# The delta rule's gates raised in priority, head 0's work scheduled right behind them, and a longer delay before its inverse

## The chip, the cores and the metric

The kernel runs on one NeuronCore of a Trainium2 chip. The metric is device time in microseconds (us), the median over executions; lower is better. Engines are named as in the profile: PE is TensorE's matmul stream, PEld its weight loads, DVE is VectorE, ACT is ScalarE, POOL is GpSimd, SP is SyncE (here it only issues DMAs).

## What is computed

A differential-attention layer, then a feed-forward block, a token mixer and a second feed-forward block, on 512 tokens of 1024 features in float32. The change lies in the token mixer, in its gated delta rule of eight heads (head size 128). The part that matters, with the sizes of this case (T = 512, H = 8):

```
proj = h @ mix_w_in                     # xp, q, k, v, z, b_raw, a_raw, g_pool, g_dn
qkv  = silu(causal_depthwise_conv([q, k, v]))          # 4 taps
beta = sigmoid(b_raw)                                  # T x H
g    = -exp(a_log) * softplus(a_raw + dt_bias)         # T x H
gc   = cumsum(g)                                       # within a chunk
decay = exp(gc_i - gc_j), lower triangle
a_mat = strict lower part of beta_i * (k_i . k_j) * decay
sol   = inverse(a_mat + I) applied to [beta*v, beta*exp(gc)*k]
for each chunk:  v_new = u - w S;  o = q_dec S + qk v_new;  S = S exp(g_last) + k_dec^T v_new
```

So every head needs the gates `beta` and `gc` of all heads, then a triangular inverse, then a scan over four chunks of 128 tokens.

## The kernel before

Everything is laid out by hand on PE: each wide product is split in high and low parts (`whi`, `wlo`, made from a `raw` weight tile by `split`, line 105: ACT casts `whi`, DVE subtracts to get `wlo`), and `mm3` issues three matmuls per 128 rows. A column of a projection (`gemm_col`, line 187) is 24 matmuls of 128x512 that write one PSUM bank. In the mixer these columns are the filler: while PE streams them, the small steps of the delta rule are put in between.

What decides the order: the class has a planner's clock, `self.now`, in us. Each matmul adds its planned time; `later(delay, fn)` puts a step on a heap, due that long after the present; `spend` runs what is due after each group of three matmuls; `run_until(cond)` runs steps at once until a condition holds. The delays are the numbers in `DL` (line 34): `cs` from the first gate steps to the cumulative sum, `U` from the solved diagonal blocks to the inverse's first level, `pr` from the end of a head's columns to that head. PE runs its instructions exactly in the order in which they are written. DVE, ACT and POOL are arranged by the library's scheduler by priority when the program is built; what `high_priority(offset=PRIO)` encloses is moved ahead of it by 200. On the chip each engine runs its row of instructions in that fixed order.

The steps that the change touches, by line:

- `ev_ba` and `ba_trans` (lines 984 to 1036): the b and a columns are turned by four small matmuls (line 992, `sc<-ident,ba`); ACT takes an exponential (998); DVE adds, inverts and clips (999 to 1004); POOL takes a power of 32 numbers per partition (1006); then 21 DVE operations on 128x32 numbers build the logarithm's series and the gate `y` (1008 to 1019). The tile is `gwork`.
- `cumsum` (1021): one small product of `y` with a triangle on PE (`sc<-gwork,cst`), copied to `gc` by DVE (1024). `rows` (1028): `gc` is turned on PE (`sc<-ident,gc`), copied (1032) and written to DRAM by a DMA that POOL issues (1033).
- `delta(h)` (1062): `decays` reads a row of that back (`row`), and makes `E` and `ET` on DVE and POOL; `products` turns k and q on PE (`sc<-ident,cvy`); POOL works out the head's factors from `ssqk` (1103 to 1110, `b` among them); `products2` multiplies k by k (`sc<-cvy`) and scales it into `E` (DVE 1119); `substitution` solves the 16x16 diagonal blocks on DVE: 15 shuffles (1153), 15 steps of `pr` and `xs` (1161, 1163), then `U` (1169). `inverse` (1175) joins blocks in three levels, each with `sc<-U,E`, a DVE step to `Q` (1186), `sc<-Q,X`, and a DVE update of `U` (1195).
- The convolution of each head's q, k and v: three DVE operations per column (1048, `cvy<-cvr,cols,cvy`).
- The loop over heads at the end of `mixer` (1317 to 1331): head 0's columns come from `gemm_quad`; `zcol(0)` and four columns of another gate (`gcol`, the "extra products", `EXTRA[0] = 4`) follow; then, for head 0 only, `run_until(gates)`, and each head is put on the heap 18 us later.

Of the kernel before, what the change touches and what calls it, by code (L numbers as in the profile page):

```python
# [15 lines left out]
P = 128  # L16
# [17 lines left out]
DL = dict(ada=21.24, qk=11.18, p0=10.0, wt=6.0, o=14.0, U=10.0, hn=7.73, lev=3.5, ch=2.2, cs=25.33, po=13.74, pr=18.0, T=3.17, la=6, gs=4, gp=5, Ts=6.12, P2=150)  # L34
# [7 lines left out]
class Net:  # L42
# [912 lines left out]
    def mixer(self):  # L955
# [33 lines left out]
        def ba_trans(ba):  # L989
# [5 lines left out]
            work = self.tile("gwork")  # L995
            e, y, m, t1, t2, ser, eb = (work[:, 32 * i:32 * i + 32].rearrange("p (h t) -> p h t", t=NT) for i in range(7))
            ea = work[:, 224:232]
            nc.scalar.activation(e, v[:, 0:8, :], AF.Exp, scale=-1.0)
            nc.vector.tensor_scalar(e, e, 1.0, None, op0=ALU.add)
            nc.vector.reciprocal(beta, e)  # L1000
# [4 lines left out]
            nc.vector.memset(eb, math.e)  # L1005
            nc.gpsimd.tensor_tensor(e, eb, t1, op=ALU.pow)

            nc.vector.tensor_scalar(t1, e, 2.0, None, op0=ALU.add)
            nc.vector.reciprocal(t2, t1)
            nc.vector.tensor_tensor(t1, e, t2, op=ALU.mult)  # L1010
# [7 lines left out]
            nc.gpsimd.tensor_tensor(ea, work[:, 192:200], alog, op=ALU.pow)  # L1018
            nc.vector.scalar_tensor_tensor(y, y, -1.0, ea.unsqueeze(2).broadcast_to([P, H, NT]), op0=ALU.mult, op1=ALU.mult)

            def cumsum():
                cs = self.bank("sc")
                self.mm(cs[:, :32], tri, fl(y))
                nc.vector.tensor_copy(fl(gc), cs[:, :32])
                nc.scalar.activation(egc, gc, AF.Exp)
                self.later(1.0, rows)

            def rows():
                tr2 = self.bank("sc")
                nc.tensor.transpose(tr2[:32, :P], fl(gc), self.ident)  # L1030
                gt = self.tile("gt")
                nc.vector.tensor_copy(gt[:32, :P], tr2[:32, :P])
                nc.gpsimd.dma_start(gdram.rearrange("h (t n) -> (h t) n", n=P), gt[:32, :P])
                st["gates"] = True

            self.later(DL["cs"], cumsum)


# [23 lines left out]
        def delta(h):  # L1062
# [75 lines left out]
            def substitution():  # L1138
# [27 lines left out]
                def expand():  # L1166
# [5 lines left out]
                    self.later(DL["U"], lambda: inverse(0))  # L1172
# [148 lines left out]
        for h in range(H):  # L1321
# [6 lines left out]
            if h == 0:  # L1328
                self.run_until(lambda: st["gates"])
            self.later(DL["pr"], lambda h=h: delta(h))  # L1330
# [120 lines left out]
```

## Time and profile before

| | |
|---|---|
| median of 3 runs | 1855.97 us (1852.57 to 1855.99) |
| the profiled execution | 1854.37 us, of which 1852.6 us are its span |
| PE busy | 1811.6 us, 98% of the span |
| DVE / ACT / POOL busy | 76% / 50% / 22% |
| the mixer's delta rule | about 960 to 1360 us of the span |

A timeline row gives the start in us, the duration, the engine, the line, the operation, the tiles as out<-in, and, in brackets, how long the engine had been idle and what released it. Neighbouring instructions of one kind are merged in a row (x2 and so on); durations of matmuls overlap, so a merged row's length is not a sum. PEclk is the granted TensorE clock: 1.00 is 2.4 GHz, 0.50 is 1.2 GHz.

### The profile page before, as it was taken

What the parts mean: (1) busy time and instruction counts of PE and PEld (TensorE: products, weight loads), DVE (VectorE), ACT (ScalarE), POOL (GpSimd) and SP (SyncE); (2) the same over time, 40 slices, a digit from 0 to 9 for tenths busy, and PEclk for the clock granted to TensorE, in tenths of its full rate; (3) what the DMA queues carried; (4) which work ended last, traced back from release to release, by engine and by line L of the source; (5) the groups of instructions that cost most, each with busy time, mean ns of one, the idle gap of its engine ahead of it and who ended that gap; (6) DMA issues with size and microseconds to landing.
All of it is one profiled execution on the core that took longest, in us unless ns stands there. A gap on an engine that the chain in (4) does not pass through costs nothing. (4 is left out here: it accounts for less than half of the span.)

```text
span 1852.6 us, 29069 instructions
## 1 busy us (share of the span) xinstructions
PE 1811.6 (98%) x10799; PEld 1598.0 (86%) x10799; DVE 1405.9 (76%) x2904; ACT 934.2 (50%) x1696; POOL 409.2 (22%) x396
## 2 busy tenths in 40 slices
PE   8999999999999999999999999999999999999997
PEld 5888888888888999998898778888888899999886
DVE  5558777777856899998365798787868789999833
ACT  5576676475743544453245745654433254445421
POOL 3213124042102123232030212212110022322201
PEclk9999999999999999999999999999999999999999
DMA  4535544535422233357324321222357323333731
GB/s 171 136 107 144 161 120 126 188 92 154 133 86 73 69 115 95 112 187 234 114 62 121 88 65 52 63 63 77 100 170 231 117 69 114 94 113 103 228 103 57
DMA packets 186594, 217.93 MB, mean 118 GB/s; under 512 B 9619, under 2 KB 129827, under 8 KB 186453
## 3 DMA queue, kind: packets, MB, share of 16 engines
q1 hardware_dynamic: 178864, 192.68, 34.6%
q0 software_dynamic: 6864, 22.27, 3.9%
q8 instruction: 85, 1.39, 0.3%
q10 hardware_dynamic: 724, 1.12, 0.2%
q14 instruction: 57, 0.46, 0.1%
HBM read 201.34 MB, written 2.11 MB: 110 GB/s over the span
## 5 line engine op out<-in xcount | busy, mean ns | idle before, releaser
L84 PE MATMUL acc<-hT,whi 128*128 128x256 f32 (+1 forms) x2704 | 639.9, 330 | 0.6 <-DVE hT L107 0.5
L84 PEld LDWEIGHTS acc<-hT,whi 128*128 128x128 f32 x2704 | 445.5, 191 | 33.4 <-DVE hT L107 0.7
L84 PE MATMUL acc<-hT,wlo 128*128 128x256 f32 (+1 forms) x1352 | 440.3, 326 | 3.0 <-DVE wlo L107 2.9
L106 ACT CAST whi<-raw 128x1024 fp32r<-128x1024 f32 (+1 forms) x325 | 285.7, 880 | 296.3 <-PE acc L84 232.2
L107 DVE TENSOR_TENSOR wlo<-raw,whi 128x1024 fp32r<-128x1024 f32 (+1 forms) x325 | 330.5, 1027 | 132.1 <-ACT whi L106 130.6
L84 PEld LDWEIGHTS acc<-hT,wlo 128*128 128x128 f32 x1352 | 257.5, 190 | 26.1 <-DVE wlo L107 4.2
L84 PE MATMUL acc<-whi,hT 128*128 128x512 f32 x768 | 264.9, 403 | 1.9 <-ACT hT L106 1.9
L84 PE MATMUL acc<-whi,gs 128*128 128x512 f32 x704 | 219.6, 390 | 1.6 <-DVE gs L107 1.6
L305 POOL TENSOR_TENSOR rs<-ms,mhalf 128x8 f32<-128x8 f32 (+2 forms) x60 | 86.2, 1438 | 447.5 <-DVE ms L303 388.0
L84 PE MATMUL acc<-T,whi 128*128 128x256 f32 x960 | 174.5, 283 | 0.0
L84 PEld LDWEIGHTS acc<-whi,hT 128*128 128x128 f32 x768 | 144.1, 188 | 32.1 <-ACT hT L106 2.9
L84 PEld LDWEIGHTS acc<-whi,gs 128*128 128x128 f32 x704 | 132.0, 188 | 29.9 <-DVE gs L107 2.5
L106 ACT CAST whi<-S 128x512 fp32r<-128x512 f32 x160 | 99.4, 621 | 115.2 <-DVE S L232 87.7
L84 PE MATMUL acc<-wlo,hT 128*128 128x512 f32 x384 | 150.5, 392 | 2.8 <-DVE wlo L584 2.8
L84 PEld LDWEIGHTS acc<-T,whi 128*128 128x128 f32 x960 | 149.8, 192 | 0.0
L107 DVE TENSOR_TENSOR wlo<-S,whi 128x512 fp32r<-128x512 f32 x160 | 140.1, 895 | 0.2 <-ACT whi L106 0.2
L84 PE MATMUL acc<-wlo,gs 128*128 128x512 f32 x352 | 137.1, 389 | 0.0
L84 PE MATMUL acc<-T,wlo 128*128 128x256 f32 x480 | 135.8, 283 | 0.0
L232 POOL TENSOR_TENSOR S<-raw,S 128x512 f32<-128x512 f32 x40 | 65.7, 1643 | 200.7 <-DVE S L232 158.6
L780 ACT ACTIVATE p<-p,mn 128x128 f32<-128x128 f32 (+3 forms) x128 | 71.1, 557 | 48.8 <-DVE mn L776 48.2
L84 PEld LDWEIGHTS acc<-T,wlo 128*128 128x128 f32 x480 | 92.2, 192 | 0.0
L84 PEld LDWEIGHTS acc<-wlo,hT 128*128 128x128 f32 x384 | 72.5, 189 | 14.7 <-DVE wlo L584 3.7
(299 smaller groups left out, 3113.6 us busy)
## 6 DMA issues: line engine op xcount, KB each, us to landing
raw<-in_ffn_w_in_dram SPq DMA_DIRECT2D x88, 512.0 KB, 3.6
raw<-in_l_w_in_dram SPq DMA_DIRECT2D x60, 512.0 KB, 4.1
raw<-in_mix_w_in_dram SPq DMA_DIRECT2D x53, 512.0 KB, 3.9
araw<-in_ada_w_dram SPq DMA_DIRECT2D x96, 256.0 KB, 4.3
raw<-in_ffn_w_out_dram SPq DMA_DIRECT2D x44, 512.0 KB, 3.7
ada<-in_ada_w_dram POOLq DMA_DIRECT2D x48, 256.0 KB, 4.2
raw<-in_l_w_out_dram SPq DMA_DIRECT2D x16, 512.0 KB, 3.7
ab<-in_ada_b_dram POOLq DMA_DIRECT2D x18, 256.0 KB, 4.2
```

Of the source, the lines that this page charges most:

```text
L84: self.nc.tensor.matmul(out, a, b, start=start, stop=stop, skip_group_check=onto)
L106: return (self.nc.scalar.copy(hi, src), self.nc.vector.tensor_tensor(lo, src, hi.bitcast(F32), op=ALU.subtract))
L107: self.nc.vector.tensor_tensor(lo, src, hi.bitcast(F32), op=ALU.subtract))
L232: sub = lambda o, x, y, op=ALU.subtract, e=nc.vector: e.tensor_tensor(o, x, y, op=op)
L305: pin(nc.gpsimd.tensor_tensor(r[:, :n], ms[:, :n], self.mhalf[:, :n], op=ALU.pow))
L780: nc.scalar.activation(p_[m][:, :L], p_[m][:, :L], AF.Exp, bias=mn[:, m:m + 1], scale=-1.0, accum_out=st[:, m, b:b + 1])
```

## The change

The gate steps of `ba_trans` become a function `logs` whose body is run at high priority; the power's result goes to a tile part of its own (`x`), so that the DVE steps for `beta` move behind the power's issue; two preparations (a memset and another power) move ahead of the projection. `cumsum` and `rows` keep their PE steps at ordinary place and get high priority for the copies. `cs` falls from 25.33 to 14.0. Head 0 no longer waits for the end of the extra products: `rows` itself puts `delta(0)` on the heap 5 us later (`d0`). Head 0's delay from solved blocks to inverse is 18 (`U0`) in place of 10. Nothing is computed anew or left out. Each old line 999 to 1019 has its counterpart at 1009 to 1028; other lines in the mixer move down by 11.

```diff
@@ -31,7 +31,7 @@
 SLOTS = 61
 PRIO = 200
 
-DL = dict(ada=21.24, qk=11.18, p0=10.0, wt=6.0, o=14.0, U=10.0, hn=7.73, lev=3.5, ch=2.2, cs=25.33, po=13.74, pr=18.0, T=3.17, la=6, gs=4, gp=5, Ts=6.12, P2=150)
+DL = dict(ada=21.24, qk=11.18, p0=10.0, wt=6.0, o=14.0, U=10.0, hn=7.73, lev=3.5, ch=2.2, cs=14.0, d0=5.0, U0=18.0, po=13.74, pr=18.0, T=3.17, la=6, gs=4, gp=5, Ts=6.12, P2=150)
 
 
 ORDER = ["M1", "M4", "M7", "M6", "M5", "M2", "M3"]
@@ -992,22 +992,32 @@
                 nc.tensor.transpose(tr[:, t * 16:(t + 1) * 16], ba[:16, sl(t)], self.ident[:16, :16])
             self.now += 0.2
             v = tr[:, :64].rearrange("p (t c) -> p c t", c=16)
-            work = self.tile("gwork")
-            e, y, m, t1, t2, ser, eb = (work[:, 32 * i:32 * i + 32].rearrange("p (h t) -> p h t", t=NT) for i in range(7))
-            ea = work[:, 224:232]
+            with self.tc.high_priority(offset=PRIO):
+                y = logs(v)
+            self.later(DL["cs"], lambda: cumsum(y))
+
+        gwork = self.tile("gwork")
+        e, y_, m, t1, t2, ser, eb = (gwork[:, 32 * i:32 * i + 32].rearrange("p (h t) -> p h t", t=NT) for i in range(7))
+        ea = gwork[:, 224:232]
+        nc.vector.memset(eb, math.e)
+        nc.gpsimd.tensor_tensor(ea, gwork[:, 192:200], alog, op=ALU.pow)
+
+        def logs(v):
+
+            y = y_
             nc.scalar.activation(e, v[:, 0:8, :], AF.Exp, scale=-1.0)
-            nc.vector.tensor_scalar(e, e, 1.0, None, op0=ALU.add)
-            nc.vector.reciprocal(beta, e)
             nc.vector.tensor_tensor(y, v[:, 8:16, :], dtb.unsqueeze(2).broadcast_to([P, H, NT]), op=ALU.add)
             nc.vector.tensor_scalar(t1, y, 0.0, None, op0=ALU.min)
             nc.vector.tensor_scalar(m, y, 0.0, None, op0=ALU.max)
             nc.vector.tensor_tensor(t1, t1, m, op=ALU.subtract)
-            nc.vector.memset(eb, math.e)
-            nc.gpsimd.tensor_tensor(e, eb, t1, op=ALU.pow)
-
-            nc.vector.tensor_scalar(t1, e, 2.0, None, op0=ALU.add)
-            nc.vector.reciprocal(t2, t1)
-            nc.vector.tensor_tensor(t1, e, t2, op=ALU.mult)
+            x = t2
+            nc.gpsimd.tensor_tensor(x, eb, t1, op=ALU.pow)
+            nc.vector.tensor_scalar(e, e, 1.0, None, op0=ALU.add)
+            nc.vector.reciprocal(beta, e)
+
+            nc.vector.tensor_scalar(t1, x, 2.0, None, op0=ALU.add)
+            nc.vector.reciprocal(e, t1)
+            nc.vector.tensor_tensor(t1, x, e, op=ALU.mult)
             nc.vector.tensor_tensor(t2, t1, t1, op=ALU.mult)
             nc.vector.tensor_scalar(ser, t2, 2.0 / 17, 2.0 / 15, op0=ALU.mult, op1=ALU.add)
             for d in (13, 11, 9, 7, 5, 3, 1):
@@ -1015,25 +1025,26 @@
                 nc.vector.tensor_scalar(ser, ser, 2.0 / d, None, op0=ALU.add)
             nc.vector.tensor_tensor(ser, ser, t1, op=ALU.mult)
             nc.vector.tensor_tensor(y, ser, m, op=ALU.add)
-            nc.gpsimd.tensor_tensor(ea, work[:, 192:200], alog, op=ALU.pow)
             nc.vector.scalar_tensor_tensor(y, y, -1.0, ea.unsqueeze(2).broadcast_to([P, H, NT]), op0=ALU.mult, op1=ALU.mult)
-
-            def cumsum():
-                cs = self.bank("sc")
-                self.mm(cs[:, :32], tri, fl(y))
+            return y
+
+        def cumsum(y):
+            cs = self.bank("sc")
+            self.mm(cs[:, :32], tri, fl(y))
+            with self.tc.high_priority(offset=PRIO):
                 nc.vector.tensor_copy(fl(gc), cs[:, :32])
                 nc.scalar.activation(egc, gc, AF.Exp)
-                self.later(1.0, rows)
-
-            def rows():
-                tr2 = self.bank("sc")
-                nc.tensor.transpose(tr2[:32, :P], fl(gc), self.ident)
-                gt = self.tile("gt")
+            self.later(1.0, rows)
+
+        def rows():
+            tr2 = self.bank("sc")
+            nc.tensor.transpose(tr2[:32, :P], fl(gc), self.ident)
+            gt = self.tile("gt")
+            with self.tc.high_priority(offset=PRIO):
                 nc.vector.tensor_copy(gt[:32, :P], tr2[:32, :P])
-                nc.gpsimd.dma_start(gdram.rearrange("h (t n) -> (h t) n", n=P), gt[:32, :P])
-                st["gates"] = True
-
-            self.later(DL["cs"], cumsum)
+            nc.gpsimd.dma_start(gdram.rearrange("h (t n) -> (h t) n", n=P), gt[:32, :P])
+            st["gates"] = True
+            self.later(DL["d0"], lambda: delta(0))
 
 
         conv_out = {}
@@ -1169,7 +1180,7 @@
                     nc.vector.tensor_tensor(U.rearrange("p (t b i) -> p t b i", t=NT, b=8), b8(xs, 2),
                                             b8(bmask.rearrange("p (b i) -> p b i", b=8), 1), op=ALU.mult)
                     d["U"] = U
-                    self.later(DL["U"], lambda: inverse(0))
+                    self.later(DL["U"] if h else DL["U0"], lambda: inverse(0))
 
                 self.later(2.0, lambda: shuffles(0))
 
@@ -1325,9 +1336,8 @@
                 zcol(h)
             for _ in range(EXTRA[h]):
                 rest.pop(0)()
-            if h == 0:
-                self.run_until(lambda: st["gates"])
-            self.later(DL["pr"], lambda h=h: delta(h))
+            if h:
+                self.later(DL["pr"], lambda h=h: delta(h))
         for f in rest[:-KD]:
             f()
         self.ada(1, 2, 2.5)
```

In the built program the rows of PE, DVE, ACT and POOL differ only in the mixer. Three places are shown.

PE, the small steps of the gates and of head 0 (`sc_..<-gwork` is the cumulative sum, `sc_..<-ident,gc` the turn of `gc`, `cvy` are k and q of a head, `U` its blocks; the wide matmuls between them are left out). Before:

```order
L84 MATMUL sc_10457<-gwork_10218,cst_10008 128x32
...
L1030 MATMUL sc_10467<-ident_75,gc_10017 32x128
...
L95 MATMUL sc_10706<-ident_75,cvy_10294 128x128 x4
L95 MATMUL sc_10716<-ident_75,cvy_10262 128x128 x4
...
L84 MATMUL sc_10762<-cvy_10294 128x128 x4
L84 MATMUL sc_10780<-cvy_10262,cvy_10294 128x128 x4
...
L95 MATMUL sc_10986<-ident_75,cvy_10578 128x128 x4
...
L84 MATMUL sc_11081<-U_10954,E_10645 128x4x16 x4
```

After:

```order
L84 MATMUL sc_10388<-gwork_10020,cst_10008 128x32
...
L1041 MATMUL sc_10398<-ident_75,gc_10017 32x128
...
L95 MATMUL sc_10509<-ident_75,cvy_10294 128x128 x4
L95 MATMUL sc_10519<-ident_75,cvy_10262 128x128 x4
...
L84 MATMUL sc_10550<-cvy_10294 128x128 x4
L84 MATMUL sc_10568<-cvy_10262,cvy_10294 128x128 x4
...
L84 MATMUL sc_10859<-U_10734,E_10438 128x4x16 x4
...
L95 MATMUL sc_11027<-ident_75,cvy_10718 128x128 x4
```

The cumulative sum stands 51 wide matmuls earlier than before, inside the first extra column in place of the third. Head 0's turns stand 57 wide matmuls behind the turn of `gc` (141 before). Between them and the first use of `U` stand 153 wide matmuls (105 before), and head 1's turns (`cvy_10718`, before `cvy_10578`) now follow that use. From head 1's turns to the first use of its own `U` there are 87 wide matmuls (93 before).

DVE, the gate chain (`gwork`) from the power's result on, with convolution taps (`cvy`) and weight splits (`wlo`) of the columns between. Before:

```order
L1004 TENSOR_TENSOR gwork_10218<-gwork_10218 128x32
L1048 SCALAR_TENSOR_TENSOR cvy_10262<-cvr_10260,cols_87,cvy_10262 128x511
L1008 TENSOR_SCALAR gwork_10218<-gwork_10218 128x32
L1048 SCALAR_TENSOR_TENSOR cvy_10262<-cvr_10260,cols_87,cvy_10262 128x510
L1009 RECIPROCAL gwork_10218<-gwork_10218 128x32
L1048 SCALAR_TENSOR_TENSOR cvy_10262<-cvr_10260,cols_87,cvy_10262 128x509
L1010 TENSOR_TENSOR gwork_10218<-gwork_10218 128x32
L107 TENSOR_TENSOR wlo_10369<-raw_10366,whi_10368 128x1024
L1011 TENSOR_TENSOR gwork_10218<-gwork_10218 128x32
L107 TENSOR_TENSOR wlo_10402<-raw_10399,whi_10401 128x1024
```

After:

```order
L1012 TENSOR_TENSOR gwork_10020<-gwork_10020 128x32
L1018 TENSOR_SCALAR gwork_10020<-gwork_10020 128x32
L1059 SCALAR_TENSOR_TENSOR cvy_10262<-cvr_10260,cols_87,cvy_10262 128x511
L1019 RECIPROCAL gwork_10020<-gwork_10020 128x32
L1059 SCALAR_TENSOR_TENSOR cvy_10262<-cvr_10260,cols_87,cvy_10262 128x510
L1020 TENSOR_TENSOR gwork_10020<-gwork_10020 128x32
L107 TENSOR_TENSOR wlo_10369<-raw_10366,whi_10368 128x1024
L1021 TENSOR_TENSOR gwork_10020<-gwork_10020 128x32
L1059 SCALAR_TENSOR_TENSOR cvy_10262<-cvr_10260,cols_87,cvy_10262 128x509
L1022 TENSOR_SCALAR gwork_10020<-gwork_10020 128x32
```

The first tap (128x511) has moved behind the step that takes the power's result (1008, now 1018). From that step to the gate's last step (1019, now 1028) the row still holds other work between the chain's steps: nine taps and four splits, where it held eight taps and four splits.

DVE, head 1's first level and the head behind it (`Q0` and `U_11241`, after `U_11279`, are head 1's; `E_11222`, after `E_11249`, and what follows it are head 2's). Before:

```order
L1119 SCALAR_TENSOR_TENSOR E_11222<-sc_11355,b2_11321,E_11222 128x128 x4
L1123 TENSOR_TENSOR ET_11223<-sc_11373,ET_11223 128x512
L1142 TENSOR_TENSOR abd_11364<-E_11222,cst_10008 128x512
L1125 TENSOR_TENSOR kd_11379<-kt_11304,ekd_11226 128x512
L1144 TENSOR_REDUCE Ac_11366<-abd_11364 128x64
L1126 TENSOR_TENSOR kt_11304<-kt_11304,bB_11322 128x512
L1186 TENSOR_TENSOR Q0_10010<-sc_11382,cst_10008 128x16x16
L1195 TENSOR_TENSOR U_10954<-U_10954,sc_11395 128x4x64
L1153 STREAM_SHUFFLE La_11368<-Ac_11366 128x64 x7
L1153 STREAM_SHUFFLE La_11369<-Ac_11366 128x64 x4
L1195 TENSOR_TENSOR U_11241<-U_11241,sc_11437 128x16x16
```

After:

```order
L1197 TENSOR_TENSOR Q0_10010<-sc_11417,cst_10008 128x16x16
L1130 SCALAR_TENSOR_TENSOR E_11249<-sc_11390,b2_11361,E_11249 128x128 x4
L1239 SCALAR_TENSOR_TENSOR S_11434<-S_11336,egl_10450,av_11432 128x128
L1153 TENSOR_TENSOR abd_11399<-E_11249,cst_10008 128x512
L1136 TENSOR_TENSOR kd_11414<-kt_11344,ekd_11253 128x512
L1155 TENSOR_REDUCE Ac_11401<-abd_11399 128x64
L1137 TENSOR_TENSOR kt_11344<-kt_11344,bB_11362 128x512
L1164 STREAM_SHUFFLE La_11403<-Ac_11401 128x64 x7
L1164 STREAM_SHUFFLE La_11404<-Ac_11401 128x64 x4
L1206 TENSOR_TENSOR U_11279<-U_11279,sc_11474 128x16x16
```

Head 1's `Q0` now stands ahead of head 2's `E` rows, and its update of `U` still behind them.

## Rows read from the trace of the kernel before

**Rows 1.** The page: busy time of each engine.

```profile
PE 1811.6 (98%) x10799; PEld 1598.0 (86%) x10799; DVE 1405.9 (76%) x2904; ACT 934.2 (50%) x1696; POOL 409.2 (22%) x396
```

**Rows 2.** Stretches of 20 us: length, busy time by engine, granted clock, DMA.

```profile
core 0: us, PE busy (x) PEld busy (x) DVE busy (x) ACT busy (x) POOL busy (x), PEclk, DMA share, GB/s
980.00:1000.00 20.00, 20.00 (x91) 16.46 (x90) 7.52 (x15) 10.55 (x13) 1.13 (x2) 1.00 0.56 146
1000.00:1020.00 20.00, 20.00 (x90) 16.56 (x89) 10.66 (x14) 10.59 (x14) 1.28 (x2) 1.00 0.35 97
1040.00:1060.00 20.00, 17.25 (x93) 14.52 (x92) 19.30 (x54) 15.56 (x23) 3.56 (x2) 0.96 0.53 143
1060.00:1080.00 20.00, 17.86 (x82) 14.77 (x81) 17.16 (x78) 8.06 (x15) 3.68 (x7) 0.87 0.19 55
1080.00:1100.00 20.00, 18.09 (x118) 15.90 (x117) 17.27 (x68) 11.92 (x22) 4.91 (x8) 1.00 0.14 41
```

**Rows 3.** PE's timeline at the waits of heads 0 and 1.

```profile
1039.27 0.50 PE L84 MATMUL acc<-hT,wlo 128*128 128x512 f32 x1 [1.01 <-DVE wlo L107]
...
1056.74 1.08 PE L84 MATMUL sc<-U,E 128*128 128x64 f32 x8 [2.68 <-DVE U L1169]
...
1059.08 1.20 PE L84 MATMUL acc<-hT,whi 128*128 128x512 f32 x2
...
1061.79 0.64 PE L84 MATMUL acc<-hT,whi 128*128 128x512 f32 x2
...
1071.20 1.22 PE L84 MATMUL sc<-U,E 128*128 128x64 f32 x8 [2.14 <-DVE U L1195]
...
1072.93 1.20 PE L84 MATMUL acc<-hT,whi 128*128 128x512 f32 x2
...
1075.57 0.62 PE L84 MATMUL acc<-hT,whi 128*128 128x512 f32 x2
...
1096.14 1.08 PE L84 MATMUL sc<-Q,X 128*128 128x64 f32 x8 [1.91 <-DVE Q L1186]
```

**Rows 4.** Two stretches of 3.4 us behind these waits, as rows 2.

```profile
1058.40:1061.80 3.40, 3.40 (x11) 2.81 (x12) 1.84 (x4) 2.02 (x4) 1.44 (x1) 0.50 0.56 154
1072.05:1075.45 3.40, 3.40 (x13) 2.92 (x13) 3.40 (x12) 0.51 (x1) 0.00 (x0) 0.50 0.54 144
```

**Rows 5.** PE's timeline at the cumulative sum.

```profile
989.18 0.30 PE L84 MATMUL sc<-gwork,cst 128*128 128x32 f32 x2
```

**Rows 6.** POOL's timeline: the power in the gate chain.

```profile
963.75 5.43 POOL L1006 TENSOR_TENSOR gwork<-gwork 128x32 f32<-128x32 f32 x1 [6.56 <-DVE gwork L1004]
```

**Rows 7.** DVE's timeline: the gate chain.

```profile
962.98 0.35 DVE L1000 RECIPROCAL beta<-gwork 128x32 f32<-128x32 f32 x1
...
963.48 0.19 DVE L1004 TENSOR_TENSOR gwork<-gwork 128x32 f32<-128x32 f32 x1
964.40 0.75 DVE L1048 SCALAR_TENSOR_TENSOR cvy<-cvr,cols,cvy 128x511 f32<-128x511 f32 x1 [0.73 <-ACT cvy L1046]
969.22 0.18 DVE L1008 TENSOR_SCALAR gwork<-gwork 128x32 f32<-128x32 f32 x1 [4.07 <-POOL gwork L1006]
969.31 0.74 DVE L1048 SCALAR_TENSOR_TENSOR cvy<-cvr,cols,cvy 128x510 f32<-128x510 f32 x1
969.97 0.35 DVE L1009 RECIPROCAL gwork<-gwork 128x32 f32<-128x32 f32 x1
...
981.82 0.19 DVE L1016 TENSOR_TENSOR gwork<-gwork 128x32 f32<-128x32 f32 x1
982.05 0.19 DVE L1017 TENSOR_TENSOR gwork<-gwork 128x32 f32<-128x32 f32 x1
982.28 0.19 DVE L1019 SCALAR_TENSOR_TENSOR gwork<-gwork 128x32 f32<-128x32 f32 x1
```

**Rows 8.** DVE's timeline: head 1's shuffles ahead of head 0's update.

```profile
1070.50 0.22 DVE L1153 STREAM_SHUFFLE La<-Ac 128x64 f32<-128x64 f32 x1
1070.63 0.19 DVE L1161 TENSOR_TENSOR pr<-La,xs 128x28 f32<-128x28 f32 x1
1070.74 0.41 DVE L1195 TENSOR_TENSOR U<-U,sc 128x256 f32<-128x256 f32 x1
```

**Rows 9.** DVE's timeline where head 2 holds head 1's step.

```profile
1088.71 0.16 DVE L1101 TENSOR_SCALAR ssqk<-ssqk 128x8 f32<-128x8 f32 x1
1091.21 1.13 DVE L1119 SCALAR_TENSOR_TENSOR E<-sc,b,E 128x128 f32<-128x128 f32 x4 [2.35 <-POOL b L1107]
...
1095.57 0.42 DVE L1186 TENSOR_TENSOR Q<-sc,cst 128x256 f32<-128x256 f32 x1
```

**Rows 10.** DVE's stretch of head 0's solve: `xs` alone, columns as rows 2.

```profile
1040.00:1056.60 16.60, 7.28 (x36) 1.00 0.59 158
```

**Rows 11.** The stretch of heads 0 to 3, as rows 2.

```profile
1040.00:1140.00 100.00, 92.67 (x549) 80.58 (x548) 87.86 (x324) 56.37 (x98) 20.87 (x27) 0.97 0.27 74
```

## The prediction

> **What bounds the kernel now.** I read the page's busy times first, then PE's waits, then the stretches in which they fall, then DVE's row there. PE is busy 98% of the span [rows 1], so a change of order can only win back what PE idles or runs slowly, or lose more. Near the change PE has four waits: 1.01 us for a weight split, 2.68 us for head 0's `U`, 2.14 us for head 0's first update of `U`, and 1.91 us for head 1's `Q` [rows 3]. Behind the second and the third the granted clock is 0.50, that is 1.2 GHz, for 3.4 us each [rows 4]. What a dip costs is read from six wide matmuls in it: from 1059.08 to 1061.79 us they take 2.71 us, from 1072.93 to 1075.57 us 2.64 us [rows 3]; at full clock a wide matmul takes 20 / 89 = 0.225 us [rows 2], so six take 1.35 us. With the small matmuls ahead of them, which are slowed likewise, I put a dip at 1.6 us. What makes PE wait is DVE: in 1040 to 1060 us it is busy 19.30 of 20 us, while in 980 to 1000 us it is busy 7.52 and in 1000 to 1020 us 10.66 [rows 2]. Head 0's solve falls into the full stretch; the slack lies 40 us earlier.
>
> **The change, part by part.**
>
> Head 0 moved forward. Between its turns and the first use of `U` stand 153 wide matmuls in place of 105: 48 x 0.225 = 10.8 us more cover. The wait was 2.68 us, so with DVE as full as before 8.1 us would be left over, and DVE is emptier there. The wait goes. The second wait came from head 1's 15 shuffles, which ran ahead of head 0's update [rows 8]; head 1's turns now stand behind head 0's first two levels, so nothing of head 1 is in that place: it goes too, with both dips. Gone: 2.68 + 2.14 + 2 x 1.6 = 8.0 us. The wait of 1.01 us was for a split queued behind head 0's shuffles [rows 3]; in the new order such a split is needed 93 wide matmuls after the turns, 20.9 us, and I count 1.0 us gone.
>
> The cumulative sum moved forward. It stands 51 wide matmuls earlier, 51 x 0.225 = 11.5 us: PE comes to it at 989.2 - 11.5 = 977.7 us [rows 5]. When is `y` ready? Before, at 982.28 + 0.19 = 982.5 us [rows 7], 6.7 us ahead of its use. The chain's first half hardly moves: POOL's power takes 5.43 us from 963.75 us [rows 6], and its issue comes earlier only by reordering the `beta` steps: the addition for `beta` and the one for `y` change places, worth about 0.1 us. Behind it, the priority does not clear DVE's row: the built order still has nine taps and four splits between the chain's steps, one tap more than before. A tap followed by a chain step costs 969.97 - 969.31 = 0.66 us [rows 7]. So `y` is ready at 982.5 + 0.66 - 0.1 = 983.0 us, and PE waits 983.0 - 977.7 = 5.3 us. Everything behind that matmul on PE waits with it, the extra columns first. A wait longer than the two that were followed by a dip should be followed by one: 5.3 + 1.6 = 6.9 us new. The ends: if the nine taps and four splits found their inputs late, 6 us and two dips, 9.2; if no dip comes, 5.3.
>
> A rule bears on the wait's size. The row: a tap with two inputs in SBUF ran at 964.40 us, inside the power, and took 0.75 us, as the next tap did outside it (0.74) [rows 6, 7]. The Trainium skill, SBUF — State Buffer, section "Who interferes with whom", says that a VectorE instruction with two SBUF inputs contends with a GpSimd instruction that reads SBUF, one of the two being held for the whole of the other. By it the power might hold 0.7 us of such waiting, the changed order would free it, and the sum would be 0.7 us lower; the tap's own row shows no hold, so I take the row.
>
> The `gc` copy, its turn and the DMA. On DVE the copies now stand directly behind `y`, and DVE then waits for PE and for the row that comes back from DRAM. Queued behind are splits of the next columns; the first is used 78 wide matmuls later, 17.6 us, so I cost that at nothing. Without this cover it would cost PE the wait for the row's DMA, a few us. ACT's exponential of `gc` likewise stands in front of evictions, which hold PSUM banks that PE needs only two columns (10.8 us) later.
>
> The longer delay (18 for 10) adds only the cover counted above. The early memset and power run on engines that idle; nothing waits for them.
>
> Heads 1 and 2. From head 1's turns to the use of its `U` there are 87 wide matmuls in place of 93, 1.4 us less, and PE no longer idles 8.0 us in between; against that DVE no longer has head 0's solve there, 7.28 us [rows 10]. About even. Head 1's other wait came from head 2's `E`, which waits 2.35 us for POOL and held head 1's `Q` from 1088.9 to 1095.6 us [rows 9]. In the new order `Q` is ahead of it and the update of `U` still behind. I keep 1.9 us; bounds 0 and 1.9 + 1.9 + 1.6 = 5.4 us.
>
> The sum, against the profiled execution of 1854.37 us: -8.0 - 1.0 + 6.9 = -2.1, so 1852.3 us. The median of the three runs is 1.6 us above that execution, so for a median 1855.97 - 2.1 = 1853.9 us.
>
> **The rivals.**
>
> B, the priority does what it says: `y` is ready by 978.7 us, at most 1 us late, and no dip follows. Then -9.0 + 1.0 = -8.0, 1848.0 us. For it: from 969.2 us the chain alone, 20 steps of 0.23 us (982.28 - 982.05) and a reciprocal, would end by 974.3 [rows 7]. Against it: the built order, in which 9 x 0.66 us of taps and 4 splits stand between.
>
> C, the stall comes, but no dip, and heads 1 and 2 run free: -9.0 + 5.3 - 1.9 = -5.6, 1850.4 us. For it: the 1.91 us wait had no dip [rows 2, 3]: the granted clock in 1080 to 1100 us is 1.00. Against it: the two waits that had one were shorter than 5.3 us.
>
> D, slower: DVE becomes the bound for heads 1 to 3. From 1040 to 1140 us DVE was busy 87.86 of 100 us and PE 92.67 [rows 11]. Taken out are PE's 8.0 us of waits and dips and DVE's 7.28 us of head 0's solve. If nothing of DVE's work leaves that stretch, because the taps and splits of the next heads, now reached earlier, fill it, then 87.9 us and some three holds of 2.35 us by POOL [rows 9], 94.9 us, stand against 92.7 - 3.2 = 89.5 us of PE: 5.4 us of new waits, two dips with them 8.6 us in place of none: -9.0 + 6.9 + 8.6 = +6.5, 1862.5 us. It turns slower than before once these waits pass 2.1 us, and measurably so past 5.8 us. For it: the 86 to 96% of DVE in 1040 to 1080 us [rows 2]. Against it: head 0's solve does leave.
>
> **How the numbers follow.** This kernel's runs spread by 0.18%, so 0.2% (3.7 us) is about what can be told from no change: between 1852.3 and 1859.7 us is "same". Forecast 0.55, B 0.08, C 0.20, D 0.17. Faster: B and C, 0.28. Slower: D, 0.17 (a part of it stays within 3.7 us, and a part of the forecast passes it; I let these cancel). The likeliest is the forecast, 1853.9 us. Its own range, with the ends of the cumulative sum and of head 1, is 1850.4 to 1859.7. The range for 8 in 10 takes in C and the milder part of D, and leaves out B and D's worst: 1849 to 1860.5 us.
>
> **What would show it.** Right: PE waits some 5 us at `sc<-gwork`, released by DVE's `gwork`, near 978 to 983 us, with a granted clock of 0.50 behind it; no wait at head 0's `sc<-U,E`; DVE below 80% in 1040 to 1060 us. Wrong: no wait at the cumulative sum (B); a wait without a dip (C); waits of PE for DVE's `U`, `Q` or `wlo` at heads 1 to 3 that sum to more than 6 us (D). A slot or bank that head 0's earlier tiles take from an eviction, which no row of before shows, would make it wrong in a way I have not priced.

## The result, and the profile after

The changed kernel takes 1865.82 us (median of 1863.07 to 1867.65) beside 1855.98 us of the kernel before: 1.0056 times as long, 95% interval 1.0044 to 1.0068. It is slower, and above the range of the prediction. The profiled execution takes 1864.93 us (span 1863.2), 10.6 us more than that of before.

The page's busy times show PE with the same 10,799 matmuls as in [rows 1], at 97% for 98%, and the other engines hardly changed:

```profile
PE 1815.6 (97%) x10799; PEld 1601.4 (86%) x10799; DVE 1409.2 (76%) x2904; ACT 930.8 (50%) x1693; POOL 407.0 (22%) x396
```

The stretches of 20 us (columns as in [rows 2]) show where PE idles: about 980 us and from 1080 to 1122 us, no longer from 1040 to 1080. The last two rows are the stretches behind the two long waits; PEclk 0.50 is 1.2 GHz.

```profile
980.00:1000.00 20.00, 17.26 (x68) 13.97 (x69) 7.15 (x18) 10.88 (x16) 3.33 (x4) 0.83 0.42 114
...
1040.00:1060.00 20.00, 20.00 (x115) 17.28 (x113) 9.31 (x15) 12.67 (x21) 1.28 (x2) 1.00 0.20 54
1080.00:1100.00 20.00, 18.33 (x119) 16.16 (x118) 17.22 (x71) 11.30 (x24) 2.67 (x6) 1.00 0.10 27
1100.00:1120.00 20.00, 17.57 (x95) 14.43 (x93) 19.21 (x68) 7.72 (x12) 3.45 (x5) 1.00 0.34 94
982.75:987.75 5.00, 5.00 (x13) 3.88 (x14) 0.47 (x2) 0.81 (x2) 0.57 (x1) 0.50 0.28 84
1122.05:1127.70 5.65, 5.65 (x27) 5.65 (x28) 3.00 (x6) 3.49 (x8) 0.00 (x0) 0.50 0.00 0
```

PE's timeline at its waits, to be read against [rows 3]. "issue" at the cumulative sum is the wait for `gwork`: the matmul starts 0.1 us after DVE's last gate step. Head 0's three levels (the first and the last stand here) have no wait. Behind them stand eight: two in head 0's own scan (`vn`, then `S`), two at head 1's second and third level, two at head 4, one each at heads 5 and 6.

```profile
982.74 0.61 PE L84 MATMUL sc<-gwork,cst 128*128 128x32 f32 x2 [5.23 <-issue]
1037.73 1.00 PE L84 MATMUL sc<-U,E 128*128 128x64 f32 x8
1058.75 1.00 PE L84 MATMUL sc<-U,E 128*128 128x64 f32 x8
1091.61 0.49 PE L84 MATMUL acc<-vn,ET 128*128 128x128 f32 x2 [1.00 <-ACT vn L1226]
1095.74 0.49 PE L84 MATMUL tr<-S,wT 128*128 128x128 f32 x2 [0.68 <-DVE S L1239]
1107.44 0.74 PE L84 MATMUL sc<-Q,X 128*128 128x64 f32 x5 [0.31 <-DVE Q L1197]
1122.03 1.97 PE L84 MATMUL sc<-Q,X 128*128 128x64 f32 x8 [4.16 <-ACT X L1201]
1224.92 0.52 PE L84 MATMUL sc<-Q,X 128*128 128x64 f32 x3 [0.80 <-DVE Q L1197]
1252.86 0.38 PE L84 MATMUL acc<-vn,ET 128*128 128x128 f32 x1 [0.75 <-ACT vn L1226]
1306.66 0.49 PE L84 MATMUL tr<-S,wT 128*128 128x128 f32 x2 [1.98 <-DVE S L1239]
1319.07 0.94 PE L84 MATMUL sc<-U,kt 128*128 128x128 f32 x6 [1.57 <-DVE U L1206]
```

PE's waits in the kernel before, beside those of [rows 3] (line, what is waited for, the sum, how often, the longest; the 2.2 us hold head 1's 1.91):

```profile
PE sc L84 <- DVE Q L1186: 2.2, 2, 1.9
PE acc L84 <- ACT vn L1215: 0.5, 1, 0.5
PE tr L84 <- DVE S L1228: 0.3, 1, 0.3
```

The sum of the two executions: head 0's three waits (a weight split, `U`, its update) and its two slow stretches are gone, 5.8 + 3.4 = 9.2 us. The cumulative sum costs 5.23 us and 5.0 us at half speed, 7.7. Head 0's scan and head 1 wait 1.00 + 0.68 + 0.31 + 4.16 = 6.15 us with 5.65 us at half speed behind it, 9.0, where before it was 0.53 + 1.91 = 2.4: 6.6 more. Heads 4 to 6 wait 0.80 + 0.75 + 1.98 + 1.57 = 5.1 us where it was 0.7: 4.4 more. That makes 9.5; a slow stretch of 3.4 us at 15 us of the span, which the execution of before did not have, adds up to 1.7. The sum is 11.2, measured are 10.6.

The longest of the waits is ACT's fixed row. PE had turned `U` by 1113.97 us. ACT's timeline (the copy `X` is what PE waits for):

```profile
1119.37 0.63 ACT L1061 ACTIVATE cvy<-cvy 128x512 f32<-128x512 f32 x1 [3.16 <-DVE cvy L1059]
1120.01 1.28 ACT L1092 ACT_TABLE_LOAD   x1
...
1121.41 0.57 ACT L1201 COPY X<-sc 128x512 f32<-128x512 f32 x1
```

A copy of 0.57 us stands behind a silu that waits 3.16 us for DVE's taps, and behind a table load for another head's exponentials. DVE is busy 19.21 of the 20 us from 1100 to 1120, so these taps are late in a full stretch of DVE. The wait of 1.98 us at 1306.66 is of the same kind on DVE: head 5's `S` (0.34 us) stands behind the block of head 7, which first waits 1.24 us for POOL:

```profile
1301.57 1.13 DVE L1130 SCALAR_TENSOR_TENSOR E<-sc,b,E 128x128 f32<-128x128 f32 x4 [1.24 <-POOL b L1118]
...
1305.93 0.41 DVE L1206 TENSOR_TENSOR U<-U,sc 128x256 f32<-128x256 f32 x1
1306.26 0.34 DVE L1239 SCALAR_TENSOR_TENSOR S<-S,egl,av 128x128 f32<-128x128 f32 x1
```

### The profile page after: what moved, and what is told of

Read it like the earlier page. It is cut to its first block, busy times and chain, and to the rows that moved or that the text cites. A ratio compares the mean times of both kernels' runs of the same rounds, so it can differ in the third digit from the quotient of the medians.

```text
span 1863.2 us, 29068 instructions
## 1 busy us (share of the span) xinstructions
PE 1815.6 (97%) x10799; PEld 1601.4 (86%) x10799; DVE 1409.2 (76%) x2904; ACT 930.8 (50%) x1693; POOL 407.0 (22%) x396
## 4 chain that ended last, share of the span: by engine, by line
PE 85%; DVE 8%; ACT 2%; issue 2%; DMA 1%; POOL 1%; POOLq 0%; SPq 0%; ACTq 0%; DVEq 0%
PE acc L84 74%; PE sc L84 5%; PE av L84 2%; DVE wlo L107 2%; PE sc L95 2%; PE tr L95 1%; PE tr L795 1%; DVE cvy L1059 1%; DVE S L232 1%; PE tr L84 1%; DVE hn L346 0%; DMA raw<-in_ffn_w_out_dram 0%; DVE pr L1172 0%; DVE T L397 0%; ACT whi L106 0%
## 5 line engine op out<-in xcount | busy, mean ns | idle before, releaser
L107 DVE TENSOR_TENSOR wlo<-raw,whi 128x1024 fp32r<-128x1024 f32 (+1 forms) x325 | 330.8, 1028 | 141.2 <-ACT whi L106 138.2
```

The costliest lines, as they stand in the source:

```text
L107: self.nc.vector.tensor_tensor(lo, src, hi.bitcast(F32), op=ALU.subtract))
```

## The experiments

Each ratio is to runs of the kernel before beside it, with its 95% interval; those runs had medians of 1853.8 to 1855.0 us. `issue_after(i)` in an edit places what it encloses behind instruction `i` in the row of its engine, without a wait.

### The two halves of the change apart

**b_cs14.** The gates' place alone, in the kernel before:

```diff
-cs=25.33
+cs=14.0
```

> The kernel before with cs = 14 for 25.33 and nothing else: the cumulative sum stands on PE where the change has it, heads 0 to 7 stand where they stood. Theory S (the stall at the cumulative sum is a cost by itself): PE waits about 5 us there, as it waited 5.2 us in the changed kernel, and a stretch at 1.2 GHz follows; in the changed kernel that stretch was 6.8 us long, of which some 5 us came after the wait, a loss of 2.5 us. Together +7.5 us against the kernel before, some 1863.5 us. Rival R (PE's pause is given back later, because the waits of 2.68 and 2.14 us at head 0 shrink when PE comes there later): at most 4.8 us and their two slow stretches come back, so 1856 to 1859 us, and the waits at head 0 are gone from the trace.

Measured: 1861.74 us, ratio 1.0039 (1.0024 to 1.0055). The waits of PE, with the line, what is waited for, the sum, how often and the longest:

```profile
PE sc L84 <- issue: 4.8, 1, 4.8
PE sc L84 <- DVE U L1169: 2.7, 1, 2.7
...
PE sc L84 <- DVE U L1195: 2.0, 1, 2.0
```

The stall is a cost by itself, 6.7 us by the medians, near theory S's 7.5. Head 0's waits are what they were: nothing of PE's pause is given back, and R falls.

**b_head0.** Head 0's part alone, in the kernel before (`cs` stays 25.33, nothing has priority):

```diff
 rows():
+    self.later(DL["d0"], lambda: delta(0))      # d0 = 5
-self.later(DL["U"], lambda: inverse(0))
+self.later(DL["U"] if h else DL["U0"], lambda: inverse(0))      # U0 = 18
-if h == 0:
-    self.run_until(lambda: st["gates"])
-self.later(DL["pr"], lambda h=h: delta(h))
+if h:
+    self.later(DL["pr"], lambda h=h: delta(h))
```

> The kernel before with head 0's part alone: head 0 starts 5 us of planned time behind the turn of gc, and its inverse has the delay of 18; cs stays 25.33 and nothing has priority. No wait at the cumulative sum is expected, and the waits of 2.68, 2.14 and 1.01 us at head 0 with two slow stretches go, 9.2 us. Theory H (heads 1 to 7 keep what they cost): 1855.0 - 9.2 = 1845.8 us. Rival A (moving head 0 re-arranges the fixed rows of ACT and DVE for all heads behind it, and that costs by itself, whatever the gates do): in the changed kernel the waits from head 1 on sum to 11.2 us where they were 2.8 in the kernel before, with one slow stretch of 2.8 us more, so 1855.0 - 9.2 + 11.2 = 1857 us.

Measured: 1854.76 us, ratio 0.9999 (0.9990 to 1.0009). PE's waits:

```profile
PE sc L84 <- DVE Q L1187: 2.0, 2, 1.9
PE tr L84 <- DVE S L1229: 1.9, 1, 1.9
PE acc L84 <- ACT vn L1216: 1.8, 1, 1.8
PE sc L84 <- ACT X L1191: 1.4, 3, 0.8
PE sc L84 <- DVE U L1196: 1.3, 2, 1.1
PE tr L84 <- DVE S L1231: 0.9, 2, 0.7
```

Neither forecast: the three waits of head 0 (2.68, 2.14, 1.01) are gone and the time is unchanged. PE's waits in the mixer sum to 9.3 us where they were 9.0 in the kernel before, now on other steps. Of these, 3.9 us (0.35, 1.10, 1.75 and 0.71) are on later steps of head 0 itself, in its levels and its scan, and 5.4 us on heads behind it. So rival A has the mechanism, except that head 0 pays a part too, and the price is smaller than in the changed kernel.

**a_U010.** The longer delay undone: `U0=10.0` for `U0=18.0` in the changed kernel.

> The changed kernel with head 0's delay before the inverse back at 10. Head 0's U is ready at 1027.5 us in the changed kernel, and PE comes to it at 1037.7 us; with 36 wide matmuls less ahead (8.1 us) it comes at 1029.6 us. Theory U (the longer delay was not needed): no wait at head 0's first level. The rows behind are arranged anew: if such an arrangement is worth some us either way, the time is off the 1865.8 us of the changed kernel by 2 to 8 us, without a wait at head 0's first U; if the longer delay was needed, a wait of 2 us or more stands there.

Measured: 1862.88 us, ratio 1.0044 (1.0027 to 1.0061); the interval overlaps that of the changed kernel. PE comes to head 0's first level at 1028.88 us and does not wait. Theory U stands: the longer delay was not needed. The rows behind were dealt anew (behind the cumulative sum the largest wait is now one of 3.06 us for a `vn` at 1164.2 us, where the changed kernel has none).

**b_pr19.** The kernel before with `pr=19.0` for `pr=18.0`.

> The kernel before with pr = 19 for 18: every head is put on the heap 1 us of planned time later, and nothing else. PE's small steps move by 3 to 9 wide matmuls, the rows of DVE and ACT are dealt anew. Theory A (an edit that moves PE's small steps re-arranges the fixed rows, and this costs or brings some us by itself): the waits of PE from head 1 on, 2.8 us in the kernel before, become 5 to 11 us, and the time is 3 to 8 us longer, 1858 to 1863 us, though the edit asks for no work and no order. Rival: the later heads have slack, an edit of this size is without effect, and the time stays within 2 us of the kernel before.

Measured: 1855.64 us, ratio 1.0012 (1.0003 to 1.0022): 1.6 us by the medians, within the rival's 2 us and less than theory A's 3 to 8. The waits sum to 10.6 us (9.0 before). From head 1 on they are 3.7 us, not the 5 to 11 of theory A. Yet the waits are others: at head 0 that for `U` grew from 2.68 to 3.65 us, that of 2.14 us for the update of `U` is gone, and one of 2.13 us for `X` is new:

```profile
1056.91 1.56 PE L84 MATMUL sc<-U,E 128*128 128x64 f32 x8 [3.65 <-DVE U L1169]
...
1066.29 1.10 PE L84 MATMUL sc<-Q,X 128*128 128x64 f32 x8 [2.13 <-ACT X L1190]
```

### The stall at the cumulative sum

In the built program the rows of PE, DVE, ACT and POOL are the same, instruction for instruction, without the high priority around `logs`, and also without all three priorities that the change adds: they did nothing here, and what moved the rows is the rest of the change. The next runs take the stall away in other ways.

**a_cs19.** In the changed kernel, a later cumulative sum with head 0 where it was:

```diff
-cs=14.0, d0=5.0
+cs=19.0, d0=0.0
```

> The changed kernel with cs = 19 for 14 and d0 = 0 for 5: the cumulative sum comes 21 wide matmuls (4.7 us) later, head 0's turns stand within one group of three wide matmuls of where they were. Theory S: of the wait of 5.2 us 0.5 us is left and the slow stretch behind it goes, a gain of 4.7 + 2.5 = 7.2 us, so 1858.6 us against 1865.8. Rival R (the pause was cover for the steps of heads 1 and 2, which come late instead): the gain is under 3 us, with waits of PE at heads 0 to 2 that are longer than the 6.1 us they sum to in the changed kernel between 1090 and 1125 us.

Measured: 1860.22 us, ratio 1.0036 (1.0022 to 1.0050). The wait is 0.47 us and the slow stretch behind it is gone, as theory S has it; but two new waits at head 0 (1.34 us at a `sc<-Q,X`, 0.48 at `sc<-U,kt`) take part of it back: from 1.0056 to 1.0036 is 3.7 us of the 7.2 forecast. PE's waits at heads 0 to 2 sum to 8.0 us, more than the 6.1 that rival R names, so this run alone does not settle it; a_clear2 below does, where the stall goes and no other wait grows.

**a_clear, a_clear2.** The taps cleared from the chain by force. In a_clear they are queued behind the last gate step, in a_clear2 behind the copy `gt`:

```diff
 ev_conv(n), for n in (0, 8, 16):
-    three taps; silu
+    with self.tc.issue_after(gate_y):      # a_clear: y's last step; a_clear2: the copy gt
+        three taps
+    silu
```

> The changed kernel with the nine convolution taps of head 0's columns queued behind the last gate step on DVE, so that the priority's aim is met by force; three splits are left between the chain's steps. PE's row is the same. Theory T (the taps between the steps hold y): the power's result comes at 968.8 us, 20 steps and three splits of 1.13 us later y is ready near 977.6 us, and PE comes to the cumulative sum at 977.5 us, so the wait is under 1 us and no slow stretch follows: 1865.8 - 5.2 - 2.5 + 0.5 = 1858.6 us. Rival P (the taps' delay is paid elsewhere: the silu behind them and the whi casts behind that in ACT's row come late, and PE waits for a weight or for head 0's cvy): the gain is under 3 us, with new waits of PE between 978 and 1000 us.

Measured: 1864.56 us, ratio 1.0051 (1.0036 to 1.0065). `y` was ready by 976.7 us, where the moved taps begin, and PE did not wait for it. It waited one step later, for the copy of `gc`, which stood behind moved taps. The time is rival P's, though not at the steps that P named. DVE's timeline and then PE's:

```profile
976.66 4.71 DVE L1054 SCALAR_TENSOR_TENSOR cvy<-cvr,cols,cvy 128x511 f32<-128x511 f32 x7
...
983.08 0.19 DVE L1035 COPY gc<-sc 128x32 f32<-128x32 f32 x1
```

```profile
977.19 0.30 PE L84 MATMUL sc<-gwork,cst 128*128 128x32 f32 x2
983.33 0.39 PE L1041 MATMUL sc<-ident,gc 128*32 128x128 f32 x1 [4.36 <-DVE gc L1035]
```

> As a_clear, but the nine taps of head 0's columns are queued behind the copy gt of the turned gc, no longer between y and the copy of gc. In a_clear the wait at the cumulative sum was gone, and PE waited 4.36 us at the next step, the turn of gc, whose input DVE copied only behind eight of the moved taps. Theory T (a row problem of DVE alone): both waits go, at most 1 us is left, no slow stretch follows, and head 0's turns at about 993 us find their cvy ready, since the taps end by 990 us: 1864.6 - 4.4 + 0.5 - 2.5 = 1858.2 us. Rival P (the work that is moved always lands in front of something that PE needs): a wait of over 2 us at head 0's turns or at a weight, 1861 us or more.

Measured: 1857.00 us, ratio 1.0016 (1.0007 to 1.0026). Both waits are gone, and nothing waits for the late taps:

```profile
976.94 0.30 PE L84 MATMUL sc<-gwork,cst 128*128 128x32 f32 x2
978.55 0.27 PE L1041 MATMUL sc<-ident,gc 128*32 128x128 f32 x1
```

From 1.0056 to 1.0016 is 0.40%, 7.4 us, against 5.23 + 2.5 = 7.7 by the profile. Theory T holds.

### The waits from head 1 on

**a_xfirst.** In the changed kernel, `X` of head 1's last level ahead of two silus and of head 3's exponentials:

```diff
+xi = nc.scalar.copy(X, xp)      # kept for h == 1, lev == 2
 the silu of columns 4, 12, 20 and exps of head 3:
+    with self.tc.issue_after(xi.ins):
```

> The changed kernel, with ACT's copy X of head 1's last level moved in ACT's row ahead of two silu activations and of head 3's exponentials with their table load; nothing else is asked for, though a few rows of later heads change places with it. Theory A (the wait of 4.16 us at 1122.03 us is ACT's fixed row: the copy stands behind a silu that waits 3.16 us for DVE's taps, and behind a table load of 1.28 us): the wait goes, and with it the slow stretch of 6.8 us behind it, a loss of 2.8 us; a gain of 7.0 us, so 1858.8 us. Rival D (DVE is the bound there, busy 19.2 of 20 us from 1100 to 1120 us; the copy only shows it): the wait moves to the next step that needs DVE, the update of U or the next Q, and the gain is under 2 us, 1864 us or more.

Measured: 1862.33 us, ratio 1.0039 (1.0024 to 1.0054). ACT's row and PE at that step:

```profile
1114.41 0.58 ACT L1218 COPY X<-sc 128x512 f32<-128x512 f32 x1
...
1117.67 0.63 ACT L1069 ACTIVATE cvy<-cvy 128x512 f32<-128x512 f32 x1 [2.15 <-DVE cvy L1060]
1118.32 1.28 ACT L1108 ACT_TABLE_LOAD   x1
```

```profile
1116.02 1.00 PE L85 MATMUL sc<-Q,X 128*128 128x64 f32 x8
...
1135.13 0.49 PE L85 MATMUL tr<-S,wT 128*128 128x128 f32 x2 [1.64 <-DVE S L1260]
```

The wait and its slow stretch are gone, as theory A has it, and it did not go to the next `U` or `Q` of these heads. But only half of the 7.0 us came: three waits of 1.64, 0.41 and 1.36 us, all for steps of DVE at heads 1 to 3, came 19 to 55 us later. Rows had changed places there too, so this run alone does not tell whether the order or a full DVE made them.

**a_both, a_clearx, a_clearx2.** This edit together with a_cs19, a_clear and a_clear2.

> Both edits together: cs = 19, d0 = 0 and the copy X of head 1's last level ahead of the silu and the exponentials. If the two costs are separate (theories S and A), the gains add: 1865.8 - 7.2 - 7.0 = 1851.6 us, which would be faster than the kernel before (1856.0) by the 4.4 us that head 0's earlier start brings. If heads 1 to 3 are bound by DVE (rival D), new waits take the place: 1856 us or more.

> a_clear with head 1's last X copy moved ahead in ACT's row as in the run a_xfirst, which took 1862.3 us. If the stall at the cumulative sum is a cost by itself, the same 7.2 us come off: 1855.1 us, about the kernel before (1855.0 beside these runs). If PE's pause there was cover for later steps, 1859 us or more.

> a_clear2 with head 1's last X copy moved ahead in ACT's row. Both causes of the two long waits are taken away, PE's row being the changed kernel's. By the sum: 1862.3 (a_xfirst) - 5.2 - 2.5 + 0.5 = 1855.1 us, level with the kernel before: what head 0's earlier start brings (9.2 us) goes to the smaller waits of heads 1 to 7, which sum to some 10 us in a_xfirst where they were 2.8 us in the kernel before. Rival: if the long waits were what delayed the later heads, those smaller waits shrink with them, and the time is under 1850 us.

Measured: 1860.52 us, 1.0024 (1.0015 to 1.0034); 1863.90, 1.0049 (1.0034 to 1.0064); 1856.12, 1.0011 (1.0001 to 1.0020). a_both misses its sum (1851.6) by far: the 4.15 us for `X` that a_cs19 has are gone, but the wait at head 0's `Q` is 1.96 us and the three waits of a_xfirst are there, and the time lies in the rival's part (1856 us or more). a_clearx keeps a_clear's wait for `gc`. a_clearx2 comes near its sum (1855.1): with both long waits away, the changed kernel is about level with the kernel before. Most of that is the stall, though. Beside a_clear2 the move of `X` brought 0.9 us, within the noise, and the waits sum to 11.0 us where they were 11.2: what left one step came back at others.

**b_h0kd, b_h0vn, b_rows, b_rows2.** Is it a lack of DVE and ACT time, or the order of the rows? These start from b_head0, without the gates' part, and each adds one move to the one before:

```diff
 b_h0kd:  products2
-    kd and kt scaled at once
+    self.later(6.0, scale_k)
 b_h0vn:  silu of column 19
+    with self.tc.issue_after(vn of head 0, chunk 0):
 b_rows:  the three steps of po, pool_branch(2)
+    with self.tc.issue_after(U of head 6, level 2):
 b_rows2: the three taps of column 4
+    with self.tc.issue_after(S of head 0, chunk 1):
```

> b_head0 (head 0's part alone, 1854.8 us) with two DVE steps of every head that nothing needs soon, the scaled copies kd and kt (0.69 us each), put 6 us of planned time later. In b_head0 four waits of PE (1.10, 0.71, 1.86 and 1.92 us) ended on a step of one head that stood in DVE's row behind the block E, ET, abd, kd, Ac, kt of the next head, and the last of them had a slow stretch behind it. Theory B (that block is the price): without kd and kt it is 1.2 to 1.3 us shorter, the four waits lose some 1.1 us each and the slow stretch goes, 4.2 + 1.5 us: 1849 us. Rival A (every such edit deals the rows anew): the four waits go or shrink, others of 1 to 2 us come in other places, and the time is within 3 us of b_head0.

Measured: 1853.40 us, ratio 0.9998 (0.9989 to 1.0008). Rival A: one wait of 3.36 us for a `vn` and one of 2.47 us for a `U` came.

> b_h0kd (1853.4 us) with one ACT instruction moved: the silu of head 3's v column, which in b_h0kd waits 1.68 us for DVE's taps with head 0's first vn behind it, is queued behind that vn. Theory R (the waits that come back behind head 0 are the order of the rows and no lack of DVE or ACT time): vn is copied at 1081.5 us in place of 1083.8, the wait of 3.36 us at acc<-vn,ET becomes 0.9, the slow stretch behind it goes (1.7 us), nothing comes elsewhere: 1853.4 - 2.5 - 1.7 = 1849.2 us. Rival A (rows dealt anew, or DVE is what holds): waits of about the same sum come at the next steps, 1852 us or more.

Measured: 1854.64 us, ratio 1.0003 (0.9995 to 1.0012). Rival A again: the wait for `vn` fell to 1.06 us, and 15 us later one of 2.92 us for head 0's `S` stood in its place.

> b_h0vn with one more move: three DVE steps of a pooling branch (po, together 1.9 us in b_h0kd, one of them 1.51) are queued behind head 6's last update of U, for which PE waited 2.47 us at 1305.3 us with a slow stretch of 3.4 us behind it. Theory R: that wait shrinks to 0.6 us and the slow stretch goes, 1.9 + 1.7 us: 1845.6 us. Rival A: a few rows behind it change places too, and waits of about the same sum come there: 1849 us or more, no better than b_h0vn.

Measured: 1852.58 us, ratio 0.9993 (0.9984 to 1.0002). The wait for head 6's `U` fell from 2.45 to 0.76 us and no wait came elsewhere, as theory R has it. The forecast time was missed, because its 1845.6 us start from the gain that b_h0vn did not bring, and it counts a slow stretch that b_h0vn does not have behind this wait; from b_h0vn's 1854.64 us, 1.7 us less is 1852.9. What was left was head 0's `S`, on DVE:

```profile
1093.93 0.74 DVE L1049 SCALAR_TENSOR_TENSOR cvy<-cvr,cols,cvy 128x511 f32<-128x511 f32 x1
...
1096.39 0.34 DVE L1245 SCALAR_TENSOR_TENSOR S<-S,egl,av 128x128 f32<-128x128 f32 x1
```

> b_rows (1852.6 us) with one more move: the three taps of head 4's q column (0.74 us each), which in b_rows stand in DVE's row ahead of head 0's state update S, are queued behind it. In b_rows PE waits 2.92 us for that S at 1096.8 us, with a slow stretch of 3.4 us behind it. Theory R (order of the rows): S is ready 2.2 us sooner, the wait is 0.7 us, the slow stretch goes: 1852.6 - 2.2 - 1.7 = 1848.7 us, faster than the kernel before by more than 0.2%. Rival A (DVE, busy 17 to 19 of 20 us there, has no time left): the taps' delay of 0.3 us or the pushed steps of head 1 give PE new waits of 2 us or more between 1097 and 1125 us, and the time stays at 1851 us or more.

Measured: 1850.00 us beside 1853.81 us, ratio 0.9980 (0.9971 to 0.9989): faster than the kernel before by 0.2%. PE at that `S` in b_rows, and then in b_rows2:

```profile
1096.78 0.49 PE L84 MATMUL tr<-S,wT 128*128 128x128 f32 x2 [2.92 <-DVE S L1245]
```

```profile
1096.57 0.49 PE L85 MATMUL tr<-S,wT 128*128 128x128 f32 x2 [0.60 <-DVE S L1253]
...
1112.11 1.10 PE L85 MATMUL sc<-Q,X 128*128 128x64 f32 x8 [0.74 <-ACT X L1211]
```

Theory R: 2.3 us of the wait and the slow stretch are gone, 0.74 us came elsewhere, and the time lies between R's 1848.7 us and rival A's 1851. So at these two steps it is the order. Over the whole stretch DVE was not short of time: from 1000 to 1140 us it is busy 108.95 us in the changed kernel and 116.55 in b_rows2, which waits less; this does not exclude that it is short for 20 us at a time, as from 1100 to 1120 us in the changed kernel. First the changed kernel's row, then that of b_rows2:

```profile
1000.00:1140.00 140.00, 133.86 (x736) 115.19 (x734) 108.95 (x373) 73.91 (x127) 19.16 (x33) 0.98 0.26 72
```

```profile
1000.00:1140.00 140.00, 134.54 (x763) 115.38 (x762) 116.55 (x401) 78.26 (x136) 23.53 (x35) 1.00 0.27 76
```

## Why the prediction was wrong

**Head 0, right.** It put 9.0 us as gone; 9.2 us went, at the places it named, and b_head0 shows them gone without the gates' part too.

**The cumulative sum, right in kind, a little too small.** It put `y` at 983.0 us and the wait at 5.3; they were 982.6 and 5.23. The priority did not clear DVE's row, as it read from the built order; it did not change the row at all. The slow stretch was put at 1.6 us, from stretches of 3.4 us [rows 4]; here 5.0 us of it lay behind the wait, a loss of 2.5. b_cs14 and a_clear2 give the whole term as 6.7 and 7.4 us for 6.9. On the one rule of the Trainium skill that was weighed (SBUF — State Buffer, "Who interferes with whom"), the trace after agrees with the row and not with the rule: with the tap moved out of it, POOL's power took 5.43 us, as in [rows 6].

**The copies of `gc` and the row's DMA, right.** PE waited for none of them.

**Heads 1 and 2, the step that failed.** The prediction's "About even" kept the 1.9 us of before, with 5.4 at the far end. Head 0's scan and head 1 came to 6.15 us of waits and 2.8 us lost in a slow stretch, 9.0 in all; 1.68 us of the waits are head 0's own scan, for which the sum had no term. The step weighed DVE's sums (1.4 us less cover, 8.0 us less pause, 7.28 us less work) and one wait that the kernel before had. The waits that came are not sums: a short copy stands behind a long wait in a fixed row, and the change had put the row in another order. The longest ended on ACT, which the step does not speak of. Heads 3 to 7 had no term at all, and heads 4 to 6 cost 4.4 us more. What head 0 gained, 9.2 us, was paid back at later steps of head 0 and at the heads behind it (b_head0: ratio 0.9999); in the changed kernel 11 us were paid. With the stall of 7.7 us that is the miss: the sum had -2.1 us, and it was +9.5.

**The rivals.** D had the sign and, at 1862.5 us, nearly the time, but for the most part by luck. Its own sign, waits for DVE's `U`, `Q` or `wlo` at heads 1 to 3 of more than 6 us, came to 0.31 us, and where single rows were moved (b_rows, b_rows2) the waits went with DVE's work unchanged. A part of it is not excluded: the longest wait stood behind DVE's taps in a stretch in which DVE was full, and in a_xfirst half of the gain went to waits for DVE. B did not come, and would not have brought its time: where the taps were cleared by force (a_clear2), it was 1857.0 us and not 1848.0, since the heads took back the gain. The range's upper end, 1860.5, left out a case that needed only the forecast's stall and the waits at head 1; the measured time needed those of heads 4 to 6 as well.

What stays open: why a given arrangement has the waits that it has. Each that was looked at is a row; that the waits of the mixer sum to 9 to 11 us in b_head0, b_h0kd, b_h0vn, b_pr19, a_clear2 and a_clearx2 alike is observed, not explained. b_h0kd and b_h0vn show that one move can fail to bring what it takes away.

## What to carry to other kernels

When an edit moves small steps on the engine that is full, the helpers' rows are dealt anew for all that follows, and what is won at the step is to be set against that: here 9 us were won, and by the profiles 8 us (b_head0) to 11 us (the changed kernel) paid. Before trusting such an edit, go through the built order for every step that the full engine takes from a helper, and look for a short instruction right behind one that waits for a third engine (a silu behind taps, a block behind a POOL power, a table load). Move that one row and time it, as in b_rows and b_rows2, and expect that some moves bring nothing, as in b_h0vn and a_clearx2. Check that a priority changes the row at all.

## What was not expected of the hardware

The stretch at 1.2 GHz behind a wait was 3.4 us long in some cases and 6.8 in others: around the ends of the waits of 5.23 and 4.16 us here they are 6.8 us, from 980.95 to 987.75 and from 1120.90 to 1127.70 us, so they begin inside the wait (the last two rows of the stretches above lie within them). Nor did the length of a wait decide alone: at the wait of 2.92 us for head 0's `S` the stretch is 6.8 us long in b_h0vn and 3.4 in b_rows, and behind the wait of 1.98 us at 1306.66 us of the changed kernel there is none, behind the same wait of 1.98 us in a_xfirst there is one. The changed kernel's row and that of a_xfirst:

```profile
1306.70:1310.00 3.30, 3.30 (x22) 3.01 (x23) 2.54 (x19) 2.31 (x7) 0.00 (x0) 1.00 0.02 5
```

```profile
1303.42:1306.80 3.38, 3.38 (x12) 2.88 (x12) 3.11 (x33) 1.77 (x6) 0.00 (x0) 0.50 0.02 5
```

Such a stretch also comes within the first 20 us of the span in some executions of several of these kernels. By an estimate, it moves what follows by up to half its length. The changed kernel's:

```profile
14.96:18.37 3.41, 3.41 (x13) 2.81 (x12) 0.56 (x1) 0.91 (x2) 0.00 (x0) 0.50 1.05 396
```
